# Token scaling, MLP weights and first vectors moved in the order of an encoder kernel

## The chip, the cores and the metric

The kernel runs on one core of one Trainium2 chip. A core has five engines that run side by side, each with an instruction queue of its own that it works through in order: TensorE (PE in the profile; PEld is its loading of the stationary operand), VectorE (DVE), ScalarE (ACT), GpSimd (POOL) and SyncE (SP), which here only starts DMA transfers. Engines wait for each other through semaphores. The metric is device time in microseconds of one execution; less is better.

## The reference, cut to what matters

One encoder layer over 1280 tokens (a prompt of 1024 and a sample of 256, which share weights but don't attend to each other), width 1024, all in float32:

```python
n = rms_norm(h, g_mix)
z = n @ w_in                          # columns: qa, ka, va, qb, kb, vb
lam = exp(sum(lambda_q1 * lambda_k1)) - exp(sum(lambda_q2 * lambda_k2)) + lam_init
oa = diff_attention(qa, ka, va, lam, slopes)      # 4 heads, two softmax maps each, ALiBi
oa = rms_norm(oa, g_subln) * (1 - lam_init)
ob = gqa_attention(rope(rms_norm(qb, g_qnorm)), rope(rms_norm(kb, g_knorm)), vb)   # 8 heads, 2 kv heads
h = h + concat(oa, ob) @ w_out
a = relu(rms_norm(h, g_mlp) @ w_ff1)              # 1024 -> 4096
h = h + (a * a) @ w_ff2                           # 4096 -> 1024
gate = sigmoid(rms_norm(h, g_ple) @ w_ple_gate)
h = h + gate * (p @ w_ple_proj)
y = rms_norm(h, g_final)
```

## The kernel before

**Products.** A float32 product is built from operands split into a high part (rounded to TensorE's fp32r form by a ScalarE copy) and a low part (what is left, a subtraction on VectorE or GpSimd). Each product is hi x hi + hi x lo + lo x hi, so every operand needs one ScalarE and one other instruction ahead of TensorE: whp and wlp for the projection weights (L177, L178), ph and pl for softmax weights (L634, L639), nhi and nlo for MLP tokens (L1114, L1115), w for MLP weights (L1080, L1081).

**Stages.** The input projection comes first: weights in pieces of 256 columns through `load_w` (raw buffers RAWB = 6, split buffers WHB = 10), tokens in 10 tiles of 128. `b_unit(2)` (keys and values of mixer B) and `va_unit(0)` are taken in turn, then `b_unit(0)` beside `va_unit(1)`, then `b_unit(1)` beside `qk_a(0)`. Between them lie the loads of some short vectors (gple, gmlp, gsub, the lambdas lam_t), the small arithmetic on lambda (lam_p, lam_e, neglam) and a transposed copy of the token norms (rp, rr_t, through DRAM as rd into R). Then the attention is laid out in rounds, with projection work for the next heads and the output projection (pso) put between its steps as filling. After the attention ends, the rest of the output projection, the norm of each token tile, its transposition and the start of the MLP run into each other. The MLP's two products use Strassen's scheme of seven products (numbers 1, 6, 7, 2, 5, 4, 3 in the order of `O1`): sums of token quarters (nb to nt, L1046) and of weight quarters (w1s, L1086 to L1098). `Unit1.put` issues the matmuls of one product for one group of 256 columns of `w_ff1`; the profile lists them at L158 with names f__ and a number. The first group is cut in two units by tokens (units n = 0 and n = 1), every later group is one unit.

**The norm of a token tile** (`mlp_norm`): the tile h is stored to DRAM (hd), since it is needed again at the end of the MLP; ScalarE takes squares of both halves with their sums (L921) into a junk buffer, a few one-column instructions form 1/rms, and the tile is scaled. For the first eight tiles in token order (`early`) ScalarE scales in place (L931), so the scale must wait until the store to hd has read h. For the last two VectorE writes the scaled tile to a buffer hn (L933). The transposes (trn, L1017) read the scaled tile, ScalarE copies them out (nb, L1025), and VectorE forms the sums. Many sums then go to their place by a copy that GpSimd's queue issues (nlo, L1032).

**First MLP weights** (`w1_load`, `w1_ops`). A group is loaded in two halves of 512 KB into slots W8 to W11, scaled by gmlp (eight GpSimd instructions, L1072) at the start of `w1_ops`, then split and summed. Slot W11 is opened only when the token buffers (`ntp`) are closed, so the second group's second half is loaded there after that.

**What sets the order.** The program text is traced in order, and a planner then places the instructions on each engine's queue by a simulated timeline, with the order of the text as priority. `issue_after(x)` adds an edge that only keeps the order on x's own engine. Loads made through `load` are chained by such edges in the order of the text. On the chip each queue is worked through in the order planned, so one instruction that waits holds all behind it.

Of the kernel before, what the change touches and what calls it, by code (L numbers as in the profile page):

```python
# [18 lines left out]
ALU = mybir.AluOpType  # L19
# [21 lines left out]
def f(ap):  # L41
    return ap.bitcast(F32)
# [3 lines left out]
def encoder_kernel(ctx: ExitStack, tc: tile.TileContext, x, xT, pT, w_in, w_out, w_ff1, w_ff2, w_gate, w_proj,  # L46
# [19 lines left out]
    INPL = 8  # L66
    HNA = (0, 1, 2, 3, 4, 5, 6, 7)
    HNX = {9: 'W5'}
# [6 lines left out]
    NBB = 6  # L75
    NTB = 2
    QB = 6
# [48 lines left out]
    def col(name, src, n):  # L126
        t = cp.tile([P, n], F32, name=name)
        load(t, src)
        return t
# [30 lines left out]
    w_dma = []  # L160
    WHB = 10
    RAWB = 6
# [23 lines left out]
    def slot(tag, shape, dt, name):  # L186
        return slot_pool[tag].tile(shape, dt, tag=tag, name=name, bufs=1)
# [207 lines left out]
    def wload(c, between={}, dma=dma):  # L395
        return load_w(w_in, c, 256, bp, bp, "p", V, between, dma)
# [24 lines left out]
    for g in gens:  # L421
        drain(g)

    gple = col("gple", g_ple, KD)
    load(gmlp, g_mlp)
# [3 lines left out]
    load(lam_t.rearrange("p a b -> p (a b)"), lams.to_broadcast([P, 256]))  # L429
    lam_p = bp.tile([P, 2, 64], F32, name="lam_p", bufs=1)  # L430
    V.tensor_tensor(lam_p, lam_t[:, 0::2, :], lam_t[:, 1::2, :], op=ALU.mult)
# [8 lines left out]
    PE.transpose(rp[:NT, :P], rstd1, ident)  # L440
    rr_t = bp.tile([NT, P], F32, name="rr_t", bufs=1)
    S.activation(rr_t, rp[:NT, :P], AF.Copy)
# [3 lines left out]

    weave(b_unit(0, wload(1536, dma=load)), va_unit(1, wload(1280, dma=load)), 1.0)
    weave(b_unit(1, wload(1792, dma=load)), qk_a(0), 1.0)
# [452 lines left out]

    norm_ends = []

    def behind_norm(fn):
# [3 lines left out]
    def mlp_norm(t):  # L908
        pos = TORD.index(t)
        j, half = divmod(pos, 2)  # L910
        h = h_row(t)
        dma(hd[half][:, j], h)
        st = cp.tile([P, 5], F32, tag=f"nst{half}", name="nst", bufs=1)
        s0, s1, u, v, rs = (st[:, i:i + 1] for i in range(5))
        early = pos < INPL
        hn[t] = (h if early else slot(HNX[pos], [P, D], F32, "hn") if pos in HNX else
                 ntp.tile([P, D], F32, tag="hn", name="hn", bufs=1))
        for n, s in enumerate((s0, s1)):
            c = slice(n * 512, n * 512 + 512)
            junk = op_state["h"][j][:, 2 * D:] if pos < 6 else ntp.tile([P, 512], F32, tag="hj", name="hj", bufs=1)  # L920
            S.activation(junk, h[:, c], AF.Square, accum_out=s)  # L921
        V.tensor_scalar(v, s0, 1.0 / D, 1e-6, op0=ALU.mult, op1=ALU.add)
        S.activation(u, s1, AF.Ln, scale=1.0 / D, bias=v)
        V.scalar_tensor_tensor(v, s1, 1.0 / D, v, op0=ALU.mult, op1=ALU.add)
        ends = [S.activation(rs, u, AF.Exp, scale=-0.5)]

        V.scalar_tensor_tensor(v, rs, rs, v, op0=ALU.mult, op1=ALU.mult)
        V.tensor_scalar(v, v, -0.5, 1.5, op0=ALU.mult, op1=ALU.add)
        if pos in HNA:
            V.tensor_tensor(rs, rs, v, op=ALU.mult)  # L930
            S.activation(hn[t], h, AF.Copy, scale=rs)  # L931
        else:
            ends.append(V.tensor_scalar(hn[t], h, rs, v, op0=ALU.mult, op1=ALU.mult))  # L933
        norm_ends[:] = ends
# [55 lines left out]
    HSLOT = {1: 0, 6: 1, 7: 2, 5: 3, 4: 5, 2: 6, 3: 4}  # L990
    open_slots(pool("fw", side="left"), ["W10"])
    LO = {i: slot(f"L{i}", [P, 4, HT], F32R, f"nlo{i}") for i in range(1, 8)}
# [9 lines left out]
    def w1_load(p, kh):  # L1002

        raw = slot(("W8", "W9", "W10", "W11")[next(w1_n) % 4], [P, 4, 256], F32, "w1r")
        dma(raw, w_ff1[kh * 512:kh * 512 + 512, p * 256:(p + 1) * 256].rearrange("(k p) c -> p k c", p=P))
        w1raw.setdefault(p, []).append(raw)

# [27 lines left out]
    DIRECT = {1: 1, 6: 2, 7: 3, 4: 3, 5: 3}  # L1035

    def mlp_sums(j):

        b11, b21, b12, b22 = (quarter.pop((j, kh, half)) for half in range(2) for kh in range(2))

        def sum_(x, y, op, n):
            if n < 2 or j == HP - 1:
                b = ntp.tile([P, 4, P], F32, tag="nt", name="nt", bufs=NTB)
            else:
                b = op_state["h"][n + 1][:, 2 * D:].rearrange("p (k t) -> p k t", t=P)
            V.tensor_tensor(b, x, y, op=op)  # L1046
            return b

        yield 1, b11
        t3 = sum_(b22, b12, ALU.subtract, 0)  # L1050
        t2 = sum_(t3, b11, ALU.add, 1)
        yield 6, t2
        yield 7, t3
        yield 4, sum_(b21, t2, ALU.subtract, 2)
        yield 5, sum_(b12, b11, ALU.subtract, 3)
        yield 2, b21
        yield 3, b22
# [9 lines left out]
    def w1_ops(p):  # L1067

        r0, r1 = w1raw.pop(p)
        for k in range(KD):  # L1070
            r = (r0, r1)[k // 4][:, k % 4]
            G.tensor_scalar(r, r, gmlp[:, k:k + 1], 1.0, op0=ALU.mult, op1=ALU.mult)  # L1072
        a11, a12, a21, a22 = r0[:, :, 0:P], r1[:, :, 0:P], r0[:, :, P:], r1[:, :, P:]
        ws = WN[p] = {}
        GS = G if p else V

# [17 lines left out]
        yield  # L1094
        s4 = slot("T2", [P, 4, P], F32, "w1s")
        GS.tensor_tensor(s4, a12, s2, op=ALU.subtract)
        s1 = slot("W2", [P, 4, P], F32, "w1s")
        GS.tensor_tensor(s1, a21, a22, op=ALU.add)  # L1098
        split(5, s1)
        yield  # L1100
        split(4, a22, GS)
        yield
        split(3, s4)
        if 0 < p < NP1 - 2:
# [4 lines left out]
    def n_split(i, c, lo_eng, src=None):  # L1109
        if src is None:  # L1110
            src = f(LO[i][:, :, c])
        if i not in HI:
            HI[i] = slot(f"H{HSLOT[i]}", [P, 4, HT], F32R, f"nhi{i}")
        S.activation(HI[i][:, :, c], src, AF.Copy)  # L1114
        lo_eng.tensor_tensor(LO[i][:, :, c], src, f(HI[i][:, :, c]), op=ALU.subtract)  # L1115

# [8 lines left out]
    for n, c in enumerate(side):  # L1125
        flush()
        if len(op_done) >= 6 and ops0 is None:
            w1_load(0, 0)
            w1_load(0, 1)
            w1_load(1, 0)  # L1130
            ops0 = w1_ops(0)
            next(ops0)
        norms()
        if c and n % 2 and steps < 2 * (len(op_done) - TLAG):
            next(trs)
            steps += 1
        if ahead and ahead[0][0] <= steps:
            ahead.pop(0)[1]()
# [104 lines left out]
    fq = pool("fq", side="left", stack=fqs)  # L1243
    open_slots(fq, ["Q2", "Q3", "W11"])
    w1_load(1, 1)
    for kh in range(2):
# [107 lines left out]
    for n, u in enumerate(units):  # L1354
        ops = w1_ops(u.p + 1) if n and u.p + 1 < NP1 else None
        for i in O1:
            if n == 0:
                n2.pop(0)()
            u.put(i)
            if ops:  # L1360
                next(ops, None)
# [46 lines left out]
    def gate_input(t):  # L1408
# [10 lines left out]
        for n in range(2):  # L1419
            jk = gq_.tile([P, 512], F32, tag="gjk", name="gjk")  # L1420
            S.activation(jk, h_half(t, n), AF.Square, accum_out=ss[:, n:n + 1])
# [159 lines left out]
```

## Time and profile before

| what | value |
|---|---|
| median of 3 runs | 1725.41 us (1723.12 to 1726.43) |
| the profiled execution | 1726.8 us, span of its instructions 1725.0 us |
| mean granted TensorE clock | 0.993 of full speed |
| busy: PE, PEld, DVE | 1674.7, 1493.8, 1173.9 us |
| busy: ACT, POOL | 860.9, 699.0 us |

All rows come from one execution. A row of a timeline gives start and length in us, engine, line, operation, the tile written and those read, shapes and how many instructions are merged; square brackets at its end give the engine's idle time before it and what ended it. A wait for several things is put down to the one that came last by the profile, so where the engine named had long been done it was another, often a DMA. Busy matmul time is modelled and also grows when the granted clock falls.

### The profile page before, as it was taken

Reading aid. Unit: us, or ns where it says so; the run is one execution under the profiler, and the core shown is the slowest. Engines: PE = TensorE matmul, PEld = TensorE weight load, DVE = VectorE, ACT = ScalarE, POOL = GpSimd, SP = SyncE. Lnnn points to the kernel's source line nnn. Section 1 sums busy time; section 2 is a strip of 40 time slices with the busy share of each in tenths; the row PEclk is TensorE's granted clock in tenths of the full one; section 3 lists DMA queues with packets and bytes.
Section 4 is the critical chain, followed back from the end, with each engine's and each line's share of the span. In section 5 each row is a group of like instructions: output and inputs, shape, how many; then the busy total and the mean of one; then the engine's idle time right before and its main releaser. Section 6 shows DMA issues by size and latency. Waiting matters only on the chain.

```text
span 1725.0 us, 27210 instructions
## 1 busy us (share of the span) xinstructions
PE 1674.7 (97%) x9849; PEld 1493.8 (87%) x9849; DVE 1173.9 (68%) x2104; ACT 860.9 (50%) x1731; POOL 699.0 (41%) x677
## 2 busy tenths in 40 slices
PE   8999999999899999898999999999999999999997
PEld 8999888888788888777999999998878888888886
DVE  7767588787788878577866666665664855355665
ACT  8532377677766667574333333333433333354554
POOL 1224455555743544535765666520433400001432
PEclk9999999999999999998999999999999999999999
DMA  9823663433953623472534333459576466532111
GB/s 318 263 83 111 202 176 122 139 90 104 271 154 117 159 84 107 121 234 81 178 125 142 136 134 129 144 171 381 194 228 192 128 203 196 169 113 77 47 43 50
DMA packets 187836, 263.60 MB, mean 153 GB/s; under 512 B 13227, under 2 KB 120629, under 8 KB 187701
## 3 DMA queue, kind: packets, MB, share of 16 engines
q1 hardware_dynamic: 185956, 256.60, 46.8%
q0 software_dynamic: 1600, 5.24, 1.1%
q8 instruction: 78, 1.28, 0.3%
q14 instruction: 58, 0.47, 0.1%
q10 hardware_dynamic: 144, 0.00, 0.0%
HBM read 175.29 MB, written 81.27 MB: 149 GB/s over the span
## 4 chain that ended last, share of the span: by engine, by line
PE 81%; DVE 6%; DMA 5%; issue 3%; ACT 3%; POOL 1%; SPq 0%; DVEq 0%; ACTq 0%; POOLq 0%
PE psg L158 6%; PE psa L242 6%; PE sc L574 6%; PE av L652 5%; PE tr L628 4%; PE pso L242 4%; PE psb L242 4%; PE psv L242 2%; PE psp L158 2%; DMA hd<-h_sb 1%; DVE pl L639 1%; DMA w2r<-in_w_ff 1%; DMA xt<-in_x 1%; PE f__15236 L158 1%; PE f__16276 L158 1%
## 5 line engine op out<-in xcount | busy, mean ns | idle before, releaser
L1290 ACT ACTIVATE ao<-ar 128x1280 fp32r<-128x1280 f32 x56 | 71.3, 1275 | 193.3 <-PE f__16280 L158 37.9
L639 DVE TENSOR_TENSOR pl<-tr,ph 128x512 fp32r<-128x512 f32 x204 | 137.9, 684 | 38.0 <-ACT ph L634 36.3
L574 PE MATMUL sc<-kt,qt 128*128 128x512 f32 (+1 forms) x576 | 156.2, 391 | 7.0 <-ACT p L599 4.6
L1292 DVE TENSOR_TENSOR ao<-ar,ao 128x1280 fp32r<-128x1280 f32 x56 | 93.3, 1667 | 100.6 <-ACT ao L1290 100.6
L634 ACT ACTIVATE ph<-tr 128x512 fp32r<-128x512 f32 x204 | 120.0, 595 | 57.0 <-PE tr L628 47.8
L242 PE MATMUL pso<-ow,mt 128*128 128x512 f32 x480 | 120.2, 396 | 3.8 <-DVE osq L679 1.3
L1072 POOL TENSOR_SCALAR w1r<-w1r,gmlp 128x256 f32<-128x256 f32 x128 | 106.0, 843 | 41.1 <-DMA w1r<-in_w_ff 27.6
L628 PE MATMUL tr<-ident,p 128*128 128x128 f32 x768 | 116.0, 274 | 6.4 <-DVE pl L639 5.8
L574 PEld LDWEIGHTS sc<-kt,qt 128*128 128x128 f32 x576 | 98.8, 189 | 25.7 <-ACT p L599 6.3
L158 PE MATMUL psg<-gw,n 128*128 128x512 f32 (+1 forms) x504 | 115.2, 384 | 0.0
L628 PEld LDWEIGHTS tr<-ident,p 128*128 128x128 f32 x768 | 91.8, 141 | 22.9 <-DVE pl L639 7.1
L158 PEld LDWEIGHTS psg<-gw,n 128*128 128x128 f32 x504 | 90.8, 188 | 19.5
L242 PEld LDWEIGHTS pso<-ow,mt 128*128 128x128 f32 x480 | 87.4, 188 | 21.7 <-DVE osq L679 1.8
L652 PE MATMUL av<-ph,vt 128*128 128x256 f32 x544 | 103.2, 291 | 1.5 <-ACT ph L634 1.0
L1080 ACT ACTIVATE w<-w1s 128x512 fp32r<-128x512 f32 x64 | 40.2, 627 | 126.5 <-POOL w1s L1086 14.3
L613 POOL TENSOR_SCALAR p<-p,rl 128x1024 f32<-128x1024 f32 x64 | 76.1, 1191 | 51.1 <-DVE rl L611 45.8
L591 DVE TENSOR_REDUCE mm<-sc 128x1 f32<-128x1024 f32 (+1 forms) x80 | 84.2, 1056 | 10.6 <-PE sc L574 10.3
L652 PE MATMUL av<-pl,vt 128*128 128x256 f32 x408 | 90.5, 303 | 0.0
L652 PEld LDWEIGHTS av<-ph,vt 128*128 128x128 f32 x544 | 83.1, 192 | 7.1 <-ACT ph L634 1.4
L599 ACT ACTIVATE p<-sc,mm 128x1024 f32<-128x1024 f32 x64 | 71.3, 1115 | 26.1 <-DVE mm L591 14.3
L1465 POOL TENSOR_TENSOR p_l<-pr,p_h 128x256 fp32r<-128x256 f32 x10 | 8.2, 819 | 186.6 <-ACT p_h L1464 183.6
L596 ACT ACTIVATE p<-p,mm 128x1024 f32<-128x1024 f32 x64 | 73.5, 1148 | 20.1 <-DVE mm L587 19.3
(1511 smaller groups left out, 4795.9 us busy)
## 6 DMA issues: line engine op xcount, KB each, us to landing
ar<-ad SPq DMA_DIRECT2D x56, 640.0 KB, 4.1
w2r<-in_w_ff SPq DMA_DIRECT2D x56, 512.0 KB, 4.4
qt<-qd SPq DMA_DIRECT2D x160, 128.0 KB, 3.0
ad<-q SPq DMA_DIRECT2D x64, 320.0 KB, 2.6
w1r<-in_w_ff SPq DMA_DIRECT2D x32, 512.0 KB, 3.9
ad<-qs SPq DMA_DIRECT2D x48, 320.0 KB, 2.2
md<-ml SPq DMA_DIRECT2D x40, 256.0 KB, 2.2
mt<-md SPq DMA_DIRECT2D x20, 512.0 KB, 5.9
```

Source lines behind the costliest of these rows:

```text
L158: PE.matmul(ps, a, b, start=start and i == 0, stop=stop and i == n - 1)
L242: PE.matmul(ps, a, b, start=i == 0, stop=i == n - 1)
L574: PE.matmul(ps[:, h0:h0 + n], shared["q"][:, cc, v, i * P:(i + 1) * P], kt[:, s0 + h0:s0 + h0 + n], start=v == 0, stop=v == 1)
L591: V.tensor_reduce(out=st["m", i][:, 0:1], in_=ps[:, :sn], axis=AX.X, op=ALU.max, negate=True)
L596: S.activation(p[:, :sn], p[:, :sn], AF.Exp, scale=-1.0, bias=st["m", i][:, cc:cc + 1], accum_out=st["l", i][:, cc:cc + 1])
L613: G.tensor_scalar(p[:, :sn], p[:, :sn], rl[:, 0:1], 1.0, op0=ALU.mult, op1=ALU.mult)
L628: PE.transpose(t[:, jj, i * P:(i + 1) * P], st["ws"][i][:, j * P:(j + 1) * P], ident)
L634: S.activation(ph, st["tr", j2], AF.Copy)
L639: V.tensor_tensor(pl, st["tr", j2], f(st["ph", j2][:]), op=ALU.subtract)
L652: PE.matmul(st["av"][:, :256], x_, y_, start=j2 == 0 and n == 0, stop=j2 == nj - 1 and n == len(pr) - 1)
L1072: G.tensor_scalar(r, r, gmlp[:, k:k + 1], 1.0, op0=ALU.mult, op1=ALU.mult)
L1292: V.tensor_tensor(ao[:, 1], a, f(ao[:, 0]), op=ALU.subtract)
```

## The change

It has four parts.

- Start: the weights of `b_unit(0)` and `va_unit(1)` are loaded and split ahead, in the text, of the short vectors, the lambda arithmetic and R. Split buffers go from 10 to 11; lam_p and rr_t take buffers of the tag sq.
- Norm: the in-place scale of an early tile is kept back in a list and issued in the next tile's `mlp_norm`, behind that tile's second square on ScalarE. The junk of later tiles goes to the hn buffers, and hj is gone.
- Weights: W11 is opened with W10, both halves of the second group are loaded once eight tiles have their projection, and the scaling by gmlp is issued with each load. `w1_ops` forms s4 and s1 in place of s3 and s2, and the second group's sums and two of its low parts go to VectorE instead of GpSimd. The freed slot T2 and one buffer in `ntp` serve nt in turn.
- Order: while the second unit (n = 1) runs, the instructions of the second group's `w1_ops` are placed behind the latest token split on ScalarE and on VectorE. In the last stage gjk has one buffer.

```diff
-    HNA = (0, 1, 2, 3, 4, 5, 6, 7)
-    NTB = 2
-    WHB = 10
+    WHB = 11
...
+    w_b0, w_va1 = wload(1536, dma=load), wload(1280, dma=load)
     gple = col("gple", g_ple, KD)
     load(gmlp, g_mlp)
     gsub = col("gsub", g_subln, 1)
...
-    lam_p = bp.tile([P, 2, 64], F32, name="lam_p", bufs=1)
+    lam_p = bp.tile([P, 4, 64], F32, tag="sq", name="lam_p")[:, :2]
...
-    rr_t = bp.tile([NT, P], F32, name="rr_t", bufs=1)
+    rr_t = bp.tile([P, 4, 64], F32, tag="sq", name="rr_t").rearrange("p h d -> p (h d)")[:NT, :P]
...
-    weave(b_unit(0, wload(1536, dma=load)), va_unit(1, wload(1280, dma=load)), 1.0)
+    weave(b_unit(0, w_b0), va_unit(1, w_va1), 1.0)
...
+    scales = []
...
-            junk = op_state["h"][j][:, 2 * D:] if pos < 6 else ntp.tile([P, 512], F32, tag="hj", name="hj", bufs=1)
-            S.activation(junk, h[:, c], AF.Square, accum_out=s)
+            junk = (op_state["h"][j][:, 2 * D:] if pos < 6 else
+                    ntp.tile([P, D], F32, tag="hn", name="hj", bufs=1)[:, c] if early else hn[t][:, c])
+            sq = S.activation(junk, h[:, c], AF.Square, accum_out=s)
...
-        if pos in HNA:
+
+        with tc.issue_after(sq.ins):
+            while scales:
+                scales.pop()()
+        if early:
             V.tensor_tensor(rs, rs, v, op=ALU.mult)
-            S.activation(hn[t], h, AF.Copy, scale=rs)
+            scales.append(lambda: S.activation(h, h, AF.Copy, scale=rs))
...
-    open_slots(pool("fw", side="left"), ["W10"])
+    open_slots(pool("fw", side="left"), ["W10", "W11"])
...
         dma(raw, w_ff1[kh * 512:kh * 512 + 512, p * 256:(p + 1) * 256].rearrange("(k p) c -> p k c", p=P))
+        for k in range(4):
+            G.tensor_scalar(raw[:, k], raw[:, k], gmlp[:, 4 * kh + k:4 * kh + k + 1], 1.0, op0=ALU.mult, op1=ALU.mult)
...
-                b = ntp.tile([P, 4, P], F32, tag="nt", name="nt", bufs=NTB)
+                b = (ntp.tile([P, 4, P], F32, tag="nt", name="nt", bufs=1) if next(nt_n) % 2 else
+                     slot("T2", [P, 4, P], F32, "nt"))
...
-        for k in range(KD):
-            r = (r0, r1)[k // 4][:, k % 4]
-            G.tensor_scalar(r, r, gmlp[:, k:k + 1], 1.0, op0=ALU.mult, op1=ALU.mult)
...
-        GS = G if p else V
+        GS = G if p > 1 else V
...
-        s4 = slot("T2", [P, 4, P], F32, "w1s")
-        GS.tensor_tensor(s4, a12, s2, op=ALU.subtract)
-        s1 = slot("W2", [P, 4, P], F32, "w1s")
-        GS.tensor_tensor(s1, a21, a22, op=ALU.add)
-        split(5, s1)
+        GS.tensor_tensor(s3, a12, s2, op=ALU.subtract)
+        GS.tensor_tensor(s2, a21, a22, op=ALU.add)
+        split(5, s2)
...
-        split(3, s4)
+        split(3, s3)
...
-        S.activation(HI[i][:, :, c], src, AF.Copy)
-        lo_eng.tensor_tensor(LO[i][:, :, c], src, f(HI[i][:, :, c]), op=ALU.subtract)
+        splits[:] = (S.activation(HI[i][:, :, c], src, AF.Copy),
+                     lo_eng.tensor_tensor(LO[i][:, :, c], src, f(HI[i][:, :, c]), op=ALU.subtract))
...
         if len(op_done) >= 6 and ops0 is None:
-            w1_load(0, 0)
-            w1_load(0, 1)
-            w1_load(1, 0)
+            for kh in range(2):
+                w1_load(0, kh)
             ops0 = w1_ops(0)
             next(ops0)
+        if len(op_done) >= 8 and 1 not in w1raw:
+            for kh in range(2):
+                w1_load(1, kh)
...
-    open_slots(fq, ["Q2", "Q3", "W11"])
-    w1_load(1, 1)
+    open_slots(fq, ["Q2", "Q3"])
...
-            if ops:
+            if ops and n == 1:
+                with tc.issue_after(splits[0].ins), tc.issue_after(splits[1].ins):
+                    next(ops, None)
+            elif ops:
                 next(ops, None)
...
-            jk = gq_.tile([P, 512], F32, tag="gjk", name="gjk")
+            jk = gq_.tile([P, 512], F32, tag="gjk", name="gjk", bufs=1)
```

More of the change, by code (lines that the diff above doesn't have):

```diff
@@ L1035, in encoder_kernel @@
     DIRECT = {1: 1, 6: 2, 7: 3, 4: 3, 5: 3}
+    nt_n = itertools.count()
     def mlp_sums(j):
@@ L1113, in n_split @@
             HI[i] = slot(f"H{HSLOT[i]}", [P, 4, HT], F32R, f"nhi{i}")
-        S.activation(HI[i][:, :, c], src, AF.Copy)
-        lo_eng.tensor_tensor(LO[i][:, :, c], src, f(HI[i][:, :, c]), op=ALU.subtract)
+        splits[:] = (S.activation(HI[i][:, :, c], src, AF.Copy),
+                     lo_eng.tensor_tensor(LO[i][:, :, c], src, f(HI[i][:, :, c]), op=ALU.subtract))
+    splits = []
     trs, steps, ops0 = transposes(), 0, None
```

## The prediction

> **What bounds the kernel now.** I read the page's engine shares first, then the waits of TensorE, then busy time and clock in short stretches around each long wait, then the engines' order of time there.
>
> ```profile
> PE 1674.7 (97%) x9849; PEld 1493.8 (87%) x9849; DVE 1173.9 (68%) x2104; ACT 860.9 (50%) x1731; POOL 699.0 (41%) x677
> ```
> ```profile
> PE f__10524 L158 <- ACT nhi L1114: 6.3, 1, 6.3
> ...
> PE av L671 <- ACT o L667: 3.5, 2, 3.0
> ...
> PE trb L325 <- DVE ro L303: 2.1, 1, 2.1
> PE f__10385 L158 <- ACT nhi L1114: 2.1, 1, 2.1
> ```
> TensorE sets the time: of the span of 1725.0 us it idles 1725.0 - 1674.7 = 50.3, so only single stalls can be won. The columns of the waits are total us, times, longest. Three of the largest lie in code that the diff touches: trb (2.1), av (3.0 of 3.5), f__10524 (6.3).
>
> A stall costs more than its idle time. Stretches: PE busy, PEld, DVE, ACT, POOL, granted clock, DMA share, GB/s.
> ```profile
> 56.00:59.00 3.00, 0.88 (x9) 0.68 (x7) 1.24 (x10) 0.69 (x3) 0.00 (x0) 0.96 0.94 322
> 59.00:62.00 3.00, 3.00 (x15) 3.00 (x16) 3.00 (x12) 1.93 (x6) 0.60 (x1) 0.50 0.89 272
> ```
> ```profile
> 715.00:720.00 5.00, 5.00 (x22) 4.71 (x23) 2.24 (x5) 2.15 (x6) 1.11 (x2) 0.50 0.38 104
> 720.00:725.00 5.00, 5.00 (x30) 4.46 (x30) 1.12 (x2) 2.74 (x6) 4.31 (x7) 0.90 0.22 70
> ...
> 745.00:750.00 5.00, 5.00 (x26) 4.13 (x25) 4.18 (x8) 4.64 (x11) 4.93 (x8) 1.00 1.03 283
> ...
> 775.00:780.00 5.00, 5.00 (x23) 4.68 (x22) 5.00 (x6) 3.94 (x8) 0.00 (x0) 0.66 0.00 0
> ...
> 795.00:800.00 5.00, 0.71 (x3) 0.71 (x4) 1.25 (x3) 1.67 (x3) 3.05 (x6) 0.61 0.00 0
> 800.00:805.00 5.00, 5.00 (x33) 5.00 (x33) 3.46 (x8) 2.08 (x4) 0.00 (x0) 0.71 0.25 69
> ```
> Behind each stall the clock is 0.5 for 3 to 6 us while TensorE is busy. Lost to it: 3 x 0.5 = 1.5 us after trb; 5 x 0.5 + 5 x 0.1 = 3.0 after av; 0.71 x 0.39 + 5 x 0.29 = 1.7 after f__10524.
>
> The page "TensorE: Matmul & The Clock Gate" of the Trainium skill (What's actually happening) lets the clock fall only after an idle window of about 3.4 us. Here 2.12 us of idle were enough, so the trace decides; by the page the first item below would be worth 2.1 and not 3.6 us.
>
> **First weights ahead of the vectors.**
> ```profile
> 57.64 0.29 DVE L431 TENSOR_TENSOR lam_p<-lam_t 128x128 f32<-128x128 f32 x1 [3.82 <-DMA lam_t<-in_lams]
> ...
> 58.51 0.29 DVE L303 TENSOR_TENSOR ro<-ra,rr 128x128 f32<-128x128 f32 x1
> ```
> ```profile
> 51.70 0.38 SPq L95 DMA_DIRECT2D lam_t<-in_lams  x1
> 52.12 2.91 SPq L95 DMA_DIRECT2D rawp<-in_w_in  x5
> ```
> ```profile
> 58.86 0.48 PE L325 MATMUL trb<-ident,ro 128*128 128x128 f32 x1 [2.12 <-DVE ro L303]
> ```
> VectorE stands 3.82 us at lam_p for a load of 5.9 us (51.70 to 57.64); ro, which needs nothing of it, is queued behind, and the transpose waits for ro. The change issues eight weight loads (four per wload) on SP ahead of gple, gmlp, gsub and lam_t, and the planner will put lam_p later. ScalarE's weight splits start earlier too. If nothing replaces the wait it brings 2.12 + 1.5 = 3.6 us. The other end: lam_t and gsub now land when VectorE is full (3.00 of 3 in 59 to 62), a wait of the same 3.8 us there holds weight splits, and the item is -3.8. The nearest row is the old one, a wait that held ro; I take 2.8, between but near the top, since the 3.8 was made by a load put directly ahead of its reader. rd and R fall behind the eight loads as well; R's first reader is a whole unit later. WHB 11 adds a buffer pair and no instruction; lam_p and rr_t in sq buffers add a wait of at most one norm_rope step, beside it.
>
> **Scale behind the next tile's squares.**
> ```profile
> 712.51 1.15 ACT L931 ACTIVATE h_sb<-h_sb,nst 128x1024 f32<-128x1024 f32 x1 [5.50 <-DMA hd<-h_sb]
> 713.56 0.58 ACT L634 ACTIVATE ph<-tr 128x512 fp32r<-128x512 f32 x1
> ...
> 739.95 1.15 ACT L931 ACTIVATE h_sb<-h_sb,nst 128x1024 f32<-128x1024 f32 x1 [1.98 <-DMA hd<-h_sb]
> 741.00 0.61 ACT L921 ACTIVATE h_sb<-h_sb 128x512 f32<-128x512 f32 x1
> ```
> ```profile
> 714.83 1.22 PE L671 MATMUL av<-osq,mean_m 128*128 128x256 f32 x2 [3.01 <-ACT o L667]
> ...
> 741.25 1.03 PE L1017 MATMUL trn<-ident,h_sb 128*128 128x128 f32 x8
> ```
> The scale overwrites the tile that a store to hd is still reading; ScalarE's queue stands 5.50 us, with ph, an attention step, and the squares osq behind it, and the matmul on osq finds TensorE idle for 3.01. In the change two squares of the next tile (0.6 us each) come first, by which time the store is through: nothing is added on ScalarE, one instruction moves. What is late next is osq itself, behind its av; I leave 0.5 us of idle. So 2.5 + 3.0 = 5.5 us. Against it: the scale ends later, for the tile at 739.95 after the square that ends near 741.7, some 1.7 us, and its transposes stand right behind it at 741.25. TensorE has output projection to fill with, and how much of the 1.7 shows depends on the planner: between 0 and 1.7 I take 1.5. The junk buffer hn in place of hj is written by ScalarE alone, in its own order: 0, covered by that. Item: 4.0, from 3.8 to 6.0.
>
> **Second MLP weights early, splits ahead of them.**
> ```profile
> 783.67 13.16 POOL L1072 TENSOR_SCALAR w1r<-w1r,gmlp 128x256 f32<-128x256 f32 x8 [13.25 <-DVE q L1209]
> ```
> ```profile
> 798.09 0.63 ACT L1080 ACTIVATE w<-w1s 128x512 fp32r<-128x512 f32 x1 [10.24 <-POOL w1s L1086]
> 798.62 1.14 ACT L1114 ACTIVATE nhi<-nt 128x512 fp32r<-128x512 f32 x2
> ```
> ```profile
> 793.60 0.69 DVE L1046 TENSOR_TENSOR nt<-nb 128x512 f32<-128x512 f32 x1
> ```
> ```profile
> 799.29 2.08 PE L158 MATMUL f__10524<-nhi,w 128*128 128x256 f32 x8 [6.33 <-ACT nhi L1114]
> ```
> Eight scalings of 13.16 us hold w1s, w1s holds a weight split on ScalarE for 10.24, and the last two token splits nhi stand behind it, though the later of the sums they split is there at 794.3. The order edge puts them first: the last is through near 794.3 + 0.6 = 794.9. TensorE ran out at 792.96, so of 6.33 idle some 1.9 stay, and as the idle of 2.1 of f__10385 was followed by a clock of 0.66, I count no clock won: 4.4 us; with it 6.1, and with no idle left 8.0.
>
> What moves: the load of the second half (512 KB, 1.8 us at 283 GB/s) enters a stretch with DMA share 1.03 (745 to 750) instead of coming after the token buffers are closed, and eight scalings enter POOL's queue, among the copies to nlo that POOL issues.
> ```profile
> 749.55 2.24 POOL L1072 TENSOR_SCALAR w1r<-w1r,gmlp 128x256 f32<-128x256 f32 x4
> 751.75 0.80 POOL L1032 DMA_DIRECT2D nlo<-nb  x1
> ```
> Beside a VectorE with gaps eight cost 2 x 2.24 = 4.5 us, in a full one 13.16. Six operations of that unit go from POOL to VectorE (0.69 each, 4.1 us), and the stretch in which that unit runs has room:
> ```profile
> 800.00:850.00 50.00, 49.33 (x329) 48.74 (x329) 40.71 (x64) 18.07 (x37) 36.35 (x36) 0.97 0.45 151
> ```
> 9.3 us of VectorE are free against 4.1, so they cost 0, and 4.1 if all stood before the unit's first matmul. s4 and s1 written in place of s3 and s2 wait for splits that stand ahead of them anyway; nt in T2 keeps two buffers; the single gjk is written by one engine in order. All 0. Later scalings are issued with their loads; TensorE is never short of them now.
>
> **Sum.** 2.8 + 4.0 + 4.4 = 11.2. The profiled execution took 1726.8 us around its span of 1725.0, 1.4 above the median of 1725.41; against its own time 1715.6, against the median 1714.2.
>
> **Rivals.**
> A, the vectors' wait moves into the weight splits: 2.8 is lost and 3.8 paid, 1714.2 + 6.6 = 1720.8. For: VectorE full from 59 on. Against: lam_p's readers are far off. It decides once lam_p waits over 1 us ahead of a split.
> B, VectorE is the bound of the MLP's start: full at 775 to 780, it gets 4.1 us more, and the 4.4 are not won: 1718.6, with the 4.1 paid 1722.7. For: those stretches; against: the free time after 800.
> C, POOL at the head of its queue: the eight scalings come ahead of the last copies to nlo and fall into the full stretch, 13.2 us instead of 4.5. TensorE then waits for copied tiles about 8.7 us and loses the 1.7 of clock: 1714.2 + 10.4 = 1724.6, no change. For: the 13.16 row; against: VectorE is at 4.18 of 5 in 745 to 750, not full.
> The Trainium skill's page "SBUF — State Buffer" (Who interferes with whom) says that a VectorE instruction with two SBUF inputs locks GpSimd's reads out for its whole length. The trace agrees (13.16 for eight, against 2.24 for four); it makes C the price of coming a little late.
> D, slower: transposes wait. The scale of each tile now hangs on the next tile's projection, and where the planner puts a tile's transposes ahead of that, TensorE stands 1.7 us and runs on at half clock for 3 (1.5 us). For six tiles that is 19.2; against 2.8 + 5.5 + 4.4 won, 1725.4 + 6.5 = 1731.9. It decides from the fourth tile on (12.8). For: the row at 741.25; against: the projection matmuls that TensorE has for filling.
>
> **Chances.** Forecast 0.50; A 0.14; B 0.10; C 0.12 (with it the case that the planner's order restores a wait of the same size); D 0.14. About 0.2% (3.5 us) is what can be told from no change, so faster 0.74, same 0.12, slower 0.14. With all top values 3.6 + 6.0 + 8.0 = 17.6 the time is 1707.8; the low end is 1707. Forecast, A and B end at 1722.7; C needs 1726. The forecast's own range is 1708 to 1719.
>
> **What would show it.** No wait of trb for ro and clock 1.00 from 56 to 62; no wait of L931 for hd; clock 1.00 from 710 to 725; scalings of the second weights before the last copies, in about 5 us; nhi ahead of the unit's w on ScalarE; f__10524's successor waiting under 2 us. Wrong if lam_p, a transpose of the tiles, or a copy to nlo appears among TensorE's causes of waiting with over 2 us.

## The result, and the profile after

| what | before | after |
|---|---|---|
| median of 7 runs each | 1723.12 us (1721.84 to 1726.43) | 1714.06 us (1711.57 to 1718.38) |
| ratio, 95% interval | | 0.9948 (0.9934 to 0.9961) |
| span of the profiled execution | 1725.0 us | 1711.7 us |
| TensorE busy, idle | 1674.7, 50.3 us | 1669.0, 42.7 us |

The changed kernel is 9.1 us faster, between 6.7 and 11.4. The two profiled executions lie 13.3 us apart, more than the medians: the profiled execution of before, 1726.8, was longer than all seven runs of the table. That matters below.

The page of the changed kernel, its engine shares, and then its waits of TensorE (columns: total us, times, longest):

```profile
PE 1669.0 (98%) x9849; PEld 1488.7 (87%) x9849; DVE 1182.8 (69%) x2110; ACT 861.9 (50%) x1731; POOL 691.6 (40%) x671
```
```profile
PE f__10395 L156 <- ACT nhi L1120: 2.7, 1, 2.7
...
PE f__10502 L156 <- ACT nhi L1120: 0.8, 1, 0.8
PE psb L240 <- DVE vbl L348: 0.7, 1, 0.7
...
PE av L670 <- ACT o L666: 0.5, 1, 0.5
```

All three waits that the prediction named are gone or small: trb for ro (2.1) no longer appears, av for o fell from 3.5 to 0.5, and the 6.3 us ahead of f__10524 are now 0.8 ahead of f__10502. A wait of 2.1 for nhi grew to 2.7. Lines have moved by a few (L1114 is L1120, L931 is L936, L1072 is L1012).

Short stretches of the changed kernel (PE busy, PEld, DVE, ACT, POOL, granted clock, DMA share, GB/s):

```profile
56.00:59.00 3.00, 3.00 (x28) 3.00 (x27) 2.36 (x11) 1.52 (x3) 0.31 (x1) 1.00 0.92 307
59.00:62.00 3.00, 3.00 (x28) 3.00 (x28) 2.55 (x7) 2.20 (x7) 1.11 (x2) 1.00 0.90 281
...
715.00:720.00 5.00, 5.00 (x24) 4.12 (x23) 2.08 (x3) 3.95 (x10) 4.77 (x7) 1.00 0.59 153
...
765.00:770.00 5.00, 4.61 (x21) 4.31 (x21) 5.00 (x6) 4.63 (x10) 0.00 (x0) 0.68 0.00 0
...
785.00:790.00 5.00, 3.93 (x31) 3.63 (x30) 5.00 (x10) 2.48 (x5) 5.00 (x7) 1.00 0.00 0
```

The clock is 1.00 where it was 0.50 (59 to 62 and 715 to 720). In 765 to 770 it is 0.68, behind the new wait of 2.7. VectorE is full there and at 785 to 790, where TensorE idles 1.07 of 5.

Two instructions at the start, each in the timeline of its engine:

```profile
65.01 0.29 DVE L430 TENSOR_TENSOR lam_p<-lam_t 128x128 f32<-128x128 f32 x1 [1.34 <-DMA lam_t<-in_lams]
```
```profile
64.78 0.20 ACT L426 ACTIVATE gsub<-gsub 128x1 f32<-128x1 f32 x1 [2.62 <-DMA gsub<-in_g_subln]
```

The vectors' wait has moved and is not gone: VectorE now stands 1.34 us for lam_t and ScalarE 2.62 for gsub, in front of copies of projection results (vbl, vl). TensorE loses the 0.7 of psb to it, and no clock.

GpSimd's timeline, the scalings of weights alone and the copies around them left out:

```profile
719.15 3.68 POOL L1012 TENSOR_SCALAR w1r<-w1r,gmlp 128x256 f32<-128x256 f32 x8
...
738.50 2.73 POOL L1012 TENSOR_SCALAR w1r<-w1r,gmlp 128x256 f32<-128x256 f32 x4
...
774.60 16.10 POOL L1012 TENSOR_SCALAR w1r<-w1r,gmlp 128x256 f32<-128x256 f32 x8 [14.22 <-DVE nt L1056]
```

The first two groups are scaled by 741.2, among the copies to nlo. The eight at 774.60 belong to the third group.

ScalarE of the changed kernel, around the last two token splits:

```profile
782.92 0.63 ACT L1087 ACTIVATE w<-w1s 128x512 fp32r<-128x512 f32 x1 [3.60 <-PE f__10466 L156]
783.76 0.63 ACT L1120 ACTIVATE nhi<-nt 128x512 fp32r<-128x512 f32 x1 [0.21 <-DVE nt L1056]
...
785.96 0.63 ACT L1087 ACTIVATE w<-w1s 128x512 fp32r<-128x512 f32 x1 [1.04 <-DVE w1s L1094]
786.70 0.63 ACT L1120 ACTIVATE nhi<-nt 128x512 fp32r<-128x512 f32 x1
```

Weight splits w of the second group still stand ahead of nhi, at least one ahead of each. The wait is gone although the order isn't the forecast one: w now waits 1.04 for its sum at most, and the sum comes from VectorE.

### The profile page after: what moved, and what is told of

Its sections match the earlier page's. It is cut to its first block, busy times and chain, and to the rows that moved or that the text cites. A ratio compares the mean times of both kernels' runs of the same rounds, so it can differ in the third digit from the quotient of the medians.

```text
span 1711.7 us, 27194 instructions
## 1 busy us (share of the span) xinstructions
PE 1669.0 (98%) x9849; PEld 1488.7 (87%) x9849; DVE 1182.8 (69%) x2110; ACT 861.9 (50%) x1731; POOL 691.6 (40%) x671
## 4 chain that ended last, share of the span: by engine, by line
PE 81%; DVE 6%; DMA 4%; ACT 3%; issue 3%; POOL 2%; SPq 1%; POOLq 0%; DVEq 0%; ACTq 0%
PE psa L240 6%; PE sc L573 5%; PE pso L240 5%; PE av L651 5%; PE psg L156 4%; PE tr L627 4%; PE psb L240 3%; PE psv L240 2%; DMA xt<-in_x 1%; PE psp L156 1%; DVE pl L638 1%; PE f__14851 L156 1%; PE f__16240 L156 1%; PE f__15200 L156 1%; PE f__16582 L156 1%
## 5 line engine op out<-in xcount | busy, mean ns | idle before, releaser
L1301 DVE TENSOR_TENSOR ao<-ar,ao 128x1280 fp32r<-128x1280 f32 x56 | 87.7, 1567 | 100.3 <-ACT ao L1299 100.3
L1012 POOL TENSOR_SCALAR w1r<-w1r,gmlp 128x256 f32<-128x256 f32 x128 | 98.8, 790 | 68.2 <-DMA w1r<-in_w_ff 45.8
L1087 ACT ACTIVATE w<-w1s 128x512 fp32r<-128x512 f32 x64 | 40.0, 628 | 133.5 <-POOL w1s L1094 64.2
L586 DVE CUSTOM_DVE_ANT_0 p<-sc,dist 128x1024 f32<-128x1024 f32 x64 | 77.6, 1218 | 8.0 <-PE sc L573 4.4
## 6 DMA issues: line engine op xcount, KB each, us to landing
qt<-qd SPq DMA_DIRECT2D x160, 128.0 KB, 3.1
```

The lines of the kernel that those rows point to most:

```text
L586: V.tensor_tensor_reduce(out=p[:, :sn], in0=ps[:, :sn], in1=dst_t[:, off:off + sn], scale=SLOPES[idx], scalar=3.0e38, op0=ALU.add, op1=ALU ...
L1012: G.tensor_scalar(raw[:, k], raw[:, k], gmlp[:, 4 * kh + k:4 * kh + k + 1], 1.0, op0=ALU.mult, op1=ALU.mult)
L1301: V.tensor_tensor(ao[:, 1], a, f(ao[:, 0]), op=ALU.subtract)
```

## The experiments

Each ratio is to the kernel before, on the same chip. A difference between two variants is given as the difference of ratios times 1723 us; where their intervals overlap it isn't told from none.

The kernel cuts into three stages by two TensorE rows: the first matmul of psa from wha (end of the start) and the last of pso (end of the output projection). For before and after, first and last start:

```profile
L242 PE MATMUL psa<-xh,wha x48: 282/397/399, 128.0 to 185.2; 128*128 128x512 f32 x32, 128*128 128x256 f32 x16
...
L242 PE MATMUL pso<-ow,mt x480: 387/390/507, 451.1 to 763.2; 128*128 128x512 f32 x160
```
```profile
L240 PE MATMUL psa<-xh,wha x48: 280/397/398, 125.5 to 182.5; 128*128 128x512 f32 x32, 128*128 128x256 f32 x16
...
L240 PE MATMUL pso<-ow,mt x480: 387/389/628, 448.9 to 753.9; 128*128 128x512 f32 x160
```

Before that is 128.0 for the start, 763.2 - 128.0 = 635.2 for the middle and 1725.0 - 763.2 = 961.8 for the end; after, 125.5, 628.4 and 957.8. The same rows of the other kernels:

| kernel | start | middle | end | median us | ratio (95%) |
|---|---|---|---|---|---|
| before | 128.0 | 635.2 | 961.8 | 1723.1 | 1 |
| e1_start | 125.6 | 632.4 | 961.4 | 1722.7 | 0.9995 (0.9986 to 1.0005) |
| e2_scale | 125.5 | 629.5 | 958.8 | 1715.6 | 0.9950 (0.9938 to 0.9963) |
| e3_weights | 126.9 | 633.9 | 959.3 | 1720.1 | 0.9978 (0.9970 to 0.9987) |
| e4_edge | 125.1 | 634.0 | 961.8 | 1722.2 | 0.9996 (0.9984 to 1.0007) |
| v4_gsvec | 127.7 | 635.4 | 955.0 | 1718.1 | 0.9964 (0.9952 to 0.9977) |
| after | 125.5 | 628.4 | 957.8 | 1714.1 | 0.9948 (0.9934 to 0.9961) |
| u1_nostart | 124.9 | 630.1 | 959.3 | 1714.4 | 0.9954 (0.9941 to 0.9967) |
| u2_nodefer | 125.3 | 633.7 | 958.7 | 1719.1 | 0.9979 (0.9970 to 0.9987) |
| u3_noedge | 124.5 | 628.5 | 958.5 | 1715.7 | 0.9958 (0.9944 to 0.9972) |
| u4_gspool | 125.6 | 629.3 | 963.1 | 1720.2 | 0.9986 (0.9978 to 0.9995) |
| v1_gslate | 124.4 | 628.8 | 964.8 | 1719.9 | 0.9978 (0.9970 to 0.9987) |
| v2_late | 124.8 | 628.8 | 958.4 | 1713.9 | 0.9944 (0.9930 to 0.9957) |

The stages come from one execution each, the medians from 5 runs or more.

### One part alone, put into the kernel before

**The start.** Weights ahead of the vectors, 11 split buffers, lam_p and rr_t in buffers of sq:

```diff
-    WHB = 10
+    WHB = 11
...
+    w_b0, w_va1 = wload(1536, dma=load), wload(1280, dma=load)
     gple = col("gple", g_ple, KD)
```

> The kernel before with the first part alone (weights of b_unit(0) and va_unit(1) ahead of the vectors, 11 split buffers, lam_p and rr_t in sq buffers). Theory of three separate stalls: the 2.1 us wait of trb and the half clock behind it go, a small wait of about 0.7 us comes instead, the first B unit starts 3 us earlier and the whole kernel gains 3 us (0.17%). Rival, that a later stage takes it back (the attention's order is set by waits on other engines): the first B unit starts 3 us earlier, but the end gains under 1 us.

Measured 0.9995: 0.9 us, not told from none. The table says why the profile of before promised more. Kernels whose start is unchanged end it at 124.9, 125.1, 125.5, 126.9, 127.7 and 128.0, mean 126.4; kernels with the change at 124.4 to 125.6, mean 125.1. By these single executions the change wins some 1.2 us on average, mostly by cutting off the late cases, and the execution that the prediction was made from was the latest of all. The six with the old start also show how the price varies: where trb waited 2.1 and 2.2 us (before and e3_weights) the granted clock fell to 0.50 behind it; where its longest wait was 1.0 to 1.6 (e4_edge, v4_gsvec, u1_nostart, e2_scale) the clock stayed at 1.00.

**The scale.** Kept back until the next tile's second square:

```diff
+        with tc.issue_after(sq.ins):
+            while scales:
+                scales.pop()()
...
-            S.activation(hn[t], h, AF.Copy, scale=rs)
+            scales.append(lambda: S.activation(h, h, AF.Copy, scale=rs))
```

> The kernel before with the second part alone: the in-place scale of an early tile behind the next tile's second square; buffers as before. Theory of separate stalls: no wait of ScalarE for hd at about 707 us, no 3.0 us idle of TensorE before the matmul on osq, clock 1.0 from 710 to 725; the last output projection matmul ends 5.5 us earlier and the kernel gains 5.5 us (0.32%). Rival, the MLP's start is bound by VectorE: the projection ends 5.5 us earlier, the wait for the last token splits grows by as much, and the kernel gains under 1.5 us. Second rival, transposes wait for the later scale: waits of the transposes on the scaled tile add up to over 3 us and the gain is under 2.5 us.

Measured 0.9950, 8.6 us: alone it isn't told from the whole change. The middle is 5.7 shorter, the wait of av is 0.5. But the end is 3.0 shorter too, though no weight instruction was touched. GpSimd's timeline of e2_scale there:

```profile
771.02 5.96 POOL L1076 TENSOR_SCALAR w1r<-w1r,gmlp 128x256 f32<-128x256 f32 x4 [4.53 <-DMA w1r<-in_w_ff]
776.96 1.57 POOL L1090 TENSOR_TENSOR w1s<-w1r 128x512 f32<-128x512 f32 x1
778.51 6.72 POOL L1076 TENSOR_SCALAR w1r<-w1r,gmlp 128x256 f32<-128x256 f32 x4
```

The sum w1s now stands behind four scalings instead of eight, as the planner laid it out. The wait of 6.3 us isn't among this kernel's waits.

**The weights with the order edge.** All of the change but the start and the deferral:

```diff
...
-            scales.append(lambda: S.activation(h, h, AF.Copy, scale=rs))
+            S.activation(h, h, AF.Copy, scale=rs)
```

(The lines are against the changed kernel; the start is put back too.)

> The kernel before with the third part alone (both halves of the second weight group early, scaling with the load, sums in place and on VectorE, order edge behind the token splits, buffers moved), without the first part and with the scale where it was. Theory of separate stalls: the 6.3 us wait for nhi falls under 2 us, the clock stays 1.0 there, and the kernel gains 4 to 6 us (0.23 to 0.35%). Rival, VectorE is full and sets the end: the wait becomes one for VectorE of 3 us or more and the gain is under 2 us.

Measured 0.9978, 3.8 us, of them 2.5 in the end stage. The three parts alone add up to 0.9 + 8.6 + 3.8 = 13.3, against 9.1 together: the scale and the weights remove the same wait. Neither kernel has the 6.3 us for nhi, or one in its place, among its waits.

**The order edge alone.**

```diff
...
-            if ops:
+            if ops and n == 1:
+                with tc.issue_after(splits[0].ins), tc.issue_after(splits[1].ins):
+                    next(ops, None)
+            elif ops:
```

> The kernel before with one edge alone: in the second unit the second group's weight operations are placed behind the last token split on ScalarE and VectorE; the load, its scaling and the slots stay as before. If the order on ScalarE is what held the last token splits, the 6.3 us wait for nhi goes as in the whole third part, but the scaling (13 us for eight) still comes late, and the first matmul of the second group waits for it instead: gain 0 to 2 us. If the early load and scaling don't matter, the gain is that of the third part, 4 to 6 us.

Measured 0.9996, not told from none. ScalarE of e4_edge:

```profile
793.17 0.63 ACT L1080 ACTIVATE w<-w1s 128x512 fp32r<-128x512 f32 x1 [9.19 <-POOL w1s L1086]
793.71 0.61 ACT L1114 ACTIVATE nhi<-nt 128x512 fp32r<-128x512 f32 x1
795.16 0.64 ACT L1114 ACTIVATE nhi<-nt 128x512 fp32r<-128x512 f32 x1 [0.84 <-DVE nt L1046]
```

The split w still stands, for 9.19 us, ahead of the last two nhi. The edge ties it to the token split that is latest in the text, and that isn't the latest on the queue.

### One part taken out of the changed kernel

**Without the start.**

```diff
-    WHB = 11
+    WHB = 10
...
-    w_b0, w_va1 = wload(1536, dma=load), wload(1280, dma=load)
...
```

> The changed kernel without its start part: the two weight loads again issued behind the vectors' loads, the lambda product in a buffer of its own. Theory (the start part is worth what it measured alone, 0.05% or 0.9 us at most): 1714.1 to 1715.0, and the start stage in the trace ends anywhere between 125 and 128 us. Rival (the prediction's term was right and is only lost among the other parts when it is done alone): 2.8 us lost, 1716.9.

Measured 0.9954 against 0.9948: 1.0 us by ratio, not told from none, and the same as alone. The rival that the 2.8 show only in company expected 1716.9 and isn't borne out at 1714.4, but the two intervals are too wide to exclude it. For the part alone 2.8 is excluded: the interval of e1_start ends at 2.4.

**Without the deferral.**

```diff
-            scales.append(lambda: S.activation(h, h, AF.Copy, scale=rs))
+            S.activation(h, h, AF.Copy, scale=rs)
```

> The changed kernel with each tile's scaling in place issued at once, as before. Theory (the deferral removes the stall on ScalarE ahead of osq whatever else is done): 5 to 6 us lost, 1719 to 1720, all of it between the first psa matmul and the last pso matmul, with TensorE idle about 3 us for ScalarE's o and the clock at 0.5 behind it. Rival (the deferral gains by the planner's other order at the end of the attention, as it did when done alone): under 3 us lost, below 1717.

Measured 0.9979: 5.3 us lost, the intervals apart. The middle gives back 633.7 - 628.4 = 5.3. The wait of TensorE in u2_nodefer, and the stretch behind it:

```profile
PE av L670 <- ACT o L666: 4.6, 2, 4.1
```
```profile
710.00:715.00 5.00, 3.17 (x13) 2.89 (x14) 2.35 (x5) 4.14 (x10) 0.00 (x0) 0.66 0.03 5
```

The mechanism is as predicted: idle time ahead of the matmul on osq, and a lowered clock. The end stage differs by only 0.9 here, because in this company the scale has nothing left to win there.

**Without the edge.**

```diff
-            if ops and n == 1:
-                with tc.issue_after(splits[0].ins), tc.issue_after(splits[1].ins):
-                    next(ops, None)
-            elif ops:
+            if ops:
```

> The changed kernel without the order edge between the token splits and the second group's last weight splits. Theory (the edge alone left the old wait of 5.2 us; what removes the wait is that the scalings are done by 741 us): no change, 1713.5 to 1715, and no wait of a weight split w for w1s over 2 us on ScalarE. Rival (the prediction: the edge is what puts nhi ahead of w): the wait returns, 4.4 us lost, 1718.5.

Measured 0.9958, 1.7 us by ratio, a little above the 1715 that was expected; the intervals overlap, so a small effect is neither shown nor excluded. The wait doesn't come back: on ScalarE of u3_noedge

```profile
784.73 0.61 ACT L1087 ACTIVATE w<-w1s 128x512 fp32r<-128x512 f32 x1
787.12 0.63 ACT L1120 ACTIVATE nhi<-nt 128x512 fp32r<-128x512 f32 x1 [1.78 <-DVE nt L1056]
```

w finds its sum ready, and nhi waits only for its own sum nt.

**The six operations back on GpSimd.**

```diff
-        GS = G if p > 1 else V
+        GS = G if p else V
```

> The changed kernel with the six operations of the second group's weights (splits and sums) on GpSimd again instead of VectorE. Theory (GpSimd hardly gets on beside a full VectorE: eight scalings took 16.1 us there): the operations take 10 us or more, a weight split waits for w1s again, TensorE idles 3 to 6 us between 785 and 800, 1717 to 1720. Rival (only the scalings' early time matters, six operations of GpSimd fit ahead of their readers): within 1 us of 1714.

Measured 0.9986: 6.5 us lost, more than by any other edit. The second group is loaded and scaled early here too, as in the changed kernel. GpSimd, and TensorE's wait, in u4_gspool:

```profile
774.58 14.15 POOL L1012 TENSOR_SCALAR w1r<-w1r,gmlp 128x256 f32<-128x256 f32 x8 [13.79 <-DMA w1r<-in_w_ff]
788.70 1.26 POOL L1093 TENSOR_TENSOR w1s<-w1r 128x512 f32<-128x512 f32 x1
```
```profile
PE f__10502 L156 <- ACT nhi L1120: 5.6, 1, 5.6
```

The sum w1s stands behind eight scalings again, although its own weights have been scaled since 741. So these eight are the third group's, and what the wait hangs on is the engine that forms the sum. This kernel has the scale, the start, the early load and the edge, and yet it is 6.2 us slower by ratio than the scale alone (e2_scale, 0.9950), the intervals apart: without the new engine for the sums, the other parts bring back a wait that the scale alone had removed.

### What the eight scalings were

That sends one back to the trace of before. SP's queue and GpSimd:

```profile
779.53 0.93 SPq L1005 DMA_DIRECT2D w1r<-in_w_ff  x2
802.40 0.37 SPq L1005 DMA_DIRECT2D w1r<-in_w_ff  x1
```
```profile
796.79 1.26 POOL L1086 TENSOR_TENSOR w1s<-w1r 128x512 f32<-128x512 f32 x1
806.26 1.84 POOL L1072 TENSOR_SCALAR w1r<-w1r,gmlp 128x256 f32<-128x256 f32 x4 [8.21 <-DMA w1r<-in_w_ff]
808.18 1.29 POOL L1087 TENSOR_TENSOR w1s<-w1r,w1s 128x512 f32<-128x512 f32 x1
```

Three halves are loaded late. Two start at 779.53, into slots that the first group has left: the third group. One starts at 802.40, is scaled at 806.26, and only then comes L1087, the first sum that reads the second group's second half. So the eight scalings at 783.67, ahead of w1s (L1086), were the third group's. The sum at L1086 reads the second group's first half alone, which was scaled by 751.8. It also needs a buffer that the first group's sums use, and VectorE of before reads that for the last time here at the latest:

```profile
783.45 0.69 DVE L1081 TENSOR_TENSOR w<-w1s,w 128x512 fp32r<-128x512 f32 x1
```

From 784.1 on the sum lacked nothing. For the 12.7 us to 796.79 it stood in the wrong queue.

**Only the engine of the sums, in the kernel before.**

```diff
-        GS = G if p else V
+        GS = G if p > 1 else V
```

> The kernel before with one edit: the six operations of the second group's weights on VectorE instead of GpSimd; load and scalings stay late. Theory (the eight scalings of 13 us hold the sums w1s wherever these are computed): the wait of nhi behind w stays at 4 us or more, within 1 us of before, 1722 to 1724. Rival (with the operations off GpSimd alone the stall goes): 1719.

Measured 0.9964: 6.2 us from one changed condition, where the theory expected 1 at most and the rival 4. The theory had the eight scalings for the second group's; this run refutes it and bears out the reading above. VectorE of v4_gsvec:

```profile
788.27 0.70 DVE L1086 TENSOR_TENSOR w1s<-w1r 128x512 f32<-128x512 f32 x1
...
805.45 0.69 DVE L1087 TENSOR_TENSOR w1s<-w1r,w1s 128x512 f32<-128x512 f32 x1 [1.16 <-POOL w1r L1072]
```

L1086 runs at 788.27 without a wait, while GpSimd is still at the eight; L1087 waits for the second half. The wait of 6.3 us is not among this kernel's waits. The end stage is 955.0, 6.8 shorter. The intervals of this single edit and of the whole weights part (e3_weights, 0.9978) overlap, so whether the early load and the rest cost anything beside it stays open.

**Later scalings late again, with the sums on GpSimd, and on VectorE.** The scalings of the third and later groups go back from the load to the place of use in the text (v1_gslate has the six operations on GpSimd besides, as u4_gspool has):

```diff
-        for k in range(4):
+        for k in range(4 if p < 2 else 0):
             G.tensor_scalar(raw[:, k], raw[:, k], gmlp[:, 4 * kh + k:4 * kh + k + 1], 1.0, op0=ALU.mult, op1=ALU.mult)
...
         r0, r1 = w1raw.pop(p)
+        for k in range(KD if p > 1 else 0):
+            r = (r0, r1)[k // 4][:, k % 4]
+            G.tensor_scalar(r, r, gmlp[:, k:k + 1], 1.0, op0=ALU.mult, op1=ALU.mult)
```

> The changed kernel with the six operations of the second group's weights on GpSimd (which took 1720.2) and the scalings of the third and later groups moved from their loads back to just ahead of their use. Theory (what held the six operations were the third group's eight scalings, 14 us at the head of GpSimd's queue): they now find GpSimd free, the wait of nhi of 5.6 us goes, 1714 to 1716; VectorE has 4 us less to do in its full stretch and it may come below 1714. Rival (GpSimd is too slow beside VectorE for these operations in any order): a wait of 3 us or more stays, 1718 to 1720.

> The changed kernel with the scalings of the third and later groups moved from their loads back to just ahead of their use; the second group's six operations stay on VectorE. Theory (in the changed kernel nobody waits for the third group's scalings, which GpSimd does between 774 and 791 us): no gain, 1714 to 1715, or up to 3 us lost when the eight scalings now stand ahead of the third group's sums near 800 us. Rival (the scalings beside the full VectorE slow it): faster by 1 us or more.

v2_late: 0.9944, the same as the changed kernel. v1_gslate: 0.9978, a wait of 5.6 stays. But neither run tells its theories apart, because the edit did not move the scalings: in v2_late they start at 774.61, in v1_gslate at 773.96. GpSimd of v1_gslate:

```profile
773.96 14.16 POOL L1082 TENSOR_SCALAR w1r<-w1r,gmlp 128x256 f32<-128x256 f32 x8 [13.77 <-DMA w1r<-in_w_ff]
788.09 1.26 POOL L1096 TENSOR_TENSOR w1s<-w1r 128x512 f32<-128x512 f32 x1
```

The planner put them where they had stood, ahead of the sum, presumably because their load had landed before the sum's buffer was free. How the six operations would do on a GpSimd that stands empty was not measured.

### The clock by itself

The prediction set 1.5 us for lost clock behind an idle time of 2.12. This kernel computes no part of the encoder: blocks of 32 matmuls with pauses between them, made by a chain on VectorE.

> No part of the encoder is computed: matmuls of 128x512 in blocks of 32 with pauses of rising length between them, made by a chain of subtractions on VectorE, zeros as output. Theory (from the traces: pauses of 0.7 and 1.5 us left the clock at 1.00, 2.1 us and more were followed by 0.50): the clock of a block falls behind every pause over some 1.5 to 2.1 us and behind none below. Rival (an idle window of 3.4 us): pauses of 2.1 to 3.3 us leave 1.00.

TensorE's timeline of v3_clock, each row one block and the pause ahead of it:

```profile
46.91 7.57 PE L103 MATMUL ps<-rhs,lhs 128*128 128x512 f32 x32 [1.68 <-DVE rhs L109]
56.49 7.57 PE L103 MATMUL ps<-rhs,lhs 128*128 128x512 f32 x32 [2.01 <-DVE rhs L109]
66.39 9.15 PE L103 MATMUL ps<-rhs,lhs 128*128 128x512 f32 x32 [2.34 <-DVE rhs L109]
78.21 7.57 PE L103 MATMUL ps<-rhs,lhs 128*128 128x512 f32 x32 [2.66 <-DVE rhs L109]
88.77 9.17 PE L103 MATMUL ps<-rhs,lhs 128*128 128x512 f32 x32 [2.99 <-DVE rhs L109]
101.25 10.43 PE L103 MATMUL ps<-rhs,lhs 128*128 128x512 f32 x32 [3.32 <-DVE rhs L109]
...
178.86 9.16 PE L103 MATMUL ps<-rhs,lhs 128*128 128x512 f32 x32 [2.01 <-DVE rhs L109]
190.36 7.57 PE L103 MATMUL ps<-rhs,lhs 128*128 128x512 f32 x32 [2.34 <-DVE rhs L109]
```

A block takes 7.57 us at full clock. After pauses of up to 1.68 us none of six was slower; of the eight from 2.01 to 2.99 three were (9.15 to 9.17, 1.6 us lost), and equal pauses went both ways; from 3.32 on all nine were (9.0 to 10.4, 1.4 to 2.9 lost). Neither the theory's sharp bound at 2 nor the rival's at 3.4 holds: between them the same pause went both ways.

Nor is 1.68 us safe in the encoder. TensorE of the changed kernel, in the attention:

```profile
445.83 1.97 PE L573 MATMUL sc<-kt,qt 128*128 128x512 f32 x4 [1.65 <-ACT p L598]
```

From 446 to 449 the granted clock is 0.50 there. In before the same wait, 1.65 at 449.43, left it at 1.00.

## Why the prediction was right, point by point

**The baseline and the sum.** The forecast of 1714.2 and the measured 1714.06 agree to 0.14 us by luck, through two errors of the same size. The three runs shown beforehand had a median of 1725.41, the seven here 1723.12: 2.3 too high. The gain was put at 11.2 and was 9.1: 2.1 too high. What was right is the side, and that the gain is several us and not 1 or 20.

**The start, 2.8: mis-sized, 0.9.** This is the term that failed. The mechanism held (trb's wait is gone, the clock is 1.00 from 56 to 62), but its price was read from one execution, the one with the latest start of the six with that code. The wait of trb is 2.1 there, 1.0 in e4_edge, 1.5 in u1_nostart. The 1.5 us of clock is no fixed loss either: of the six executions with the old start, two lost it, and in v3_clock the clock fell after three of the eight pauses from 2.01 to 2.99. Rival A came true in small, as the rows of lam_p and gsub show, for 0.7 us of TensorE.

**The scale, 4.0: right, and somewhat low.** 5.3 by u2_nodefer. The 5.5 that the prediction worked out before it took 1.5 off for late transposes was the better number. Rival D, the transposes, did not happen: no trn is among the waits over 1 us after the change.

**The weights and the edge, 4.4: the wait gone, the reason wrong.** The end stage is 4.0 shorter, but 3.0 of that came in e2_scale too, with no weight instruction touched: the scale alone (8.6) isn't told from the whole change (9.1), so on top of it the weights aren't shown to win anything. The terms were added as if each had a stall of its own. And the step "Eight scalings of 13.16 us hold w1s" was read as if the second group's own weights were late, so the gain was given to the early load and to the edge that "puts them first". The edge alone isn't told from none (e4_edge), and w stands ahead of both last nhi in the changed kernel too. "Six operations of that unit go from POOL to VectorE ... so they cost 0" is the edit of this part that removes the wait: 6.2 us alone, 6.5 when taken back. The load rows of before tell the groups apart; the prediction doesn't use them.

**Rivals B and C.** VectorE is full from 765 to 790, as B said, and TensorE idles beside it, but it is not what the wait was made of: four more us of VectorE work there won time. C's price was real (eight scalings took 16.1 us in the full stretch) and its place wrong: the last copies to nlo had gone out by 760.4, and once the sums had left that queue no wait of TensorE over 1 us goes back to the third group's scalings.

**The list of signs.** One failed, the one that hung on the edge: nhi ahead of the unit's w. One came true in the main: of ScalarE's waits of the scale for hd, 11.1 us in four, one of 0.8 is left. The others came true; scalings of the second weights took 4.6 us (two, two and four), and f__10502, which stands in f__10524's place, waits 0.8.

## What to carry to other kernels

When an instruction waits for a result, look first at what stands ahead of the producer on its engine's queue, and whose work that is: here a sum that lacked nothing stood 12.7 us behind eight scalings for the next group, and changing the engine won 6.2 us, while the early load without that change (u4_gspool) left the wait at 5.6. Price a stall from several executions where its cause is a DMA's arrival; a profile shows one draw. Parts that each remove the same wait don't add: measure them alone and taken out, and believe neither number by itself.

## What the runs showed of the hardware

GpSimd's eight scalings of 128x256 took 3.68 us at 719.15 in the changed kernel, and 16.10 at 774.60, where VectorE was busy 5.00 of 5, most of it with two-input operations; VectorE's own 128x512 subtractions mostly stayed at 0.69 there. At 719.15 it was VectorE that stood back:

```profile
720.09 2.38 DVE L925 SCALAR_TENSOR_TENSOR nst<-nst 128x1 f32<-128x1 f32 x1 [0.43 <-ACT nst L924]
```

This one-column instruction takes 0.15 elsewhere (760.88); here it ends only at 722.47, close to the end of the eight at 722.83. The Trainium skill's page "SBUF — State Buffer" (Who interferes with whom) has a VectorE instruction with two inputs in SBUF and a GpSimd instruction that reads SBUF take turns on a shared port pair, a whole instruction at a time. The trace agrees that they hold each other up, in either direction; that it is these ports, no run here shows.

In v3_clock the clock fell after all nine pauses of TensorE from 3.32 us on, after three of the eight from 2.01 to 2.99, and after none of the six up to 1.68; in the encoder it fell after one of 1.65 and stayed after another of 1.65. The Trainium skill's page "TensorE: Matmul & The Clock Gate" (What's actually happening) has a free-running window of 3.4 us. That equal pauses went both ways agrees with a window that runs free; its length doesn't fit, since pauses of 1.65, 2.01, 2.34 and 2.99 us were enough. An estimate from these pauses, if a free-running window it is: 1.65 must hold a whole one, and 2.99 less than two, so some 1.5 to 1.65 us. No run here tests that.
